# The opening of the first feed-forward stage: operand blocks one at a time, and both modulation vectors summed on the tensor engine

## The chip, the cores and the metric

The kernel runs on one core of a Trainium2 chip, in one launch. Its time is the device time of that launch in microseconds (us), the median of three runs. Five engines work side by side, each through a queue of its own in a fixed order, and wait for one another by semaphores: PE (TensorE, matrix products; its weight loads are shown as PEld), DVE (VectorE), ACT (ScalarE), POOL (GpSimd) and SP, which here issues the transfers (DMA) from the chip's memory.

## The reference

One residual block (feed-forward, mixer, feed-forward, modulated by a condition vector `c`) is followed by two layers of another kind. Only the beginning matters here, up to the first products of the first feed-forward stage, `swiglu`:

```python
cond = jax.nn.silu(c)                                   # 1 x 1024
mod = cond @ w_ada[l] + b_ada[l]                        # 9 vectors of 1024
sh1, sc1, gt1, ... = split(mod, 9)
u = modulate(rmsnorm(h, g_norm_ffn1), sh1, sc1)         # rmsnorm(h) * (1 + sc1) + sh1
h = h + 0.5 * gt1 * swiglu(u, w_ffn1_in, w_ffn1_out)    # 256 tokens, 1024 -> 2 x 2816 -> 1024
```

`w_ada` is 1024 x 9216: each of its nine vectors takes 4 MB of weights, all read once.

## The kernel before

**Layout.** The tokens (256) lie along the free axis, the 1024 features in 8 blocks `k` of 128 partitions: `hT[:, k]` is 128 x 256. A 32-bit product is made of three products of split operands: every operand `x` becomes `hi = round(x)` (ACT, `S.copy`) and `lo = x - hi` (DVE), and `mm3` adds `hi*hi`, `hi*lo` and `lo*hi` in PSUM (lines 249 to 251). `split` (line 254) is that pair. Weights are `hl` (hi and lo halves), activations `xh`, `xl`.

**The first feed-forward stage** (`ffn`) multiplies `u` by `w_ffn1_in`, in 11 column blocks `j` of 2 x 256 columns. Each `j` has two sums in PSUM (`pp[j][s]`), and after the last `k`: ACT makes `sa = silu(a)`, DVE `g = b * sa`, and `split` makes `gh`, `gl`. For `j` of 3 and above the weights come as two 1 MB tiles (`raw`, five buffers) and are split in four pieces of 128 x 1024 (`hl`, six buffers).

**The opening** (`begin`) is different, since at the start nothing is there yet: the transfers of `c`, `x` and weights, the norm of `x` and the first two modulation vectors (shift `ada(0)`, scale `ada(1)`) all stand ahead of the first product. It takes the first three column blocks `j` = 0, 1, 2 together, in six PSUM banks (named `mm` for `j` = 0 and `first` for 1 and 2), and walks over the feature blocks in five groups, `CUTS` = (0), (1, 2), (3, 4), (5, 6), (7). For a group, `prepare` does the following, a group ahead of its products: shift by PE (`ada(0)`: eight matmuls at line 334 with 32 identical columns each, a copy by ACT, then the sum of the four rows by one matmul for a block at line 343), scale by DVE (`ada(1)`: one multiply with a running sum over 128 x 1024 for each block, line 354), `u = hT * r` (DVE), `u * (1+scale) + shift` (ACT), `split` of `u`, and the split of three weight pieces. `r` is the reciprocal root of the mean square of each token, made by `first_rstd`.

**What sets the order.** The code is written in the order of the program, and a scheduler of the kernel's language reorders it for each engine when it is built. `tc.issue_after(x)` keeps what follows behind `x`. On the chip the order of each engine's queue is then fixed. The transfers all go through SP's queue, and wait there for a free buffer. `busy(n)` are products of an identity that nobody reads.

Of the kernel before, what the change touches and what calls it, by code (L numbers as in the profile page):

```python
# [8 lines left out]
F32 = mybir.dt.float32  # L9
F32R = mybir.dt.float32r  # L10
BF16 = mybir.dt.bfloat16
# [95 lines left out]
def _cols(v):  # L107

    return np.ascontiguousarray(np.asarray(v).reshape(-1, P).T)
# [9 lines left out]
def layout(inputs):  # L119
# [5 lines left out]
    o["c_cols"] = _cols(a["c"])  # L125
    o["positions"] = np.ascontiguousarray(a["positions"])
    o["w_ada0"] = _panels(a["w_ada"][0][:, :D], P)
    o["w_ada1"] = np.ascontiguousarray(a["w_ada"][0].T[D:2 * D].reshape(KB, P, D))
    o["w_ada"] = np.ascontiguousarray(
        a["w_ada"][0].T[2 * D:].reshape(7, 4, 2, P, D).transpose(0, 1, 3, 2, 4))  # L130
    o["b_ada"] = _cols(a["b_ada"][0])
    o["gains"] = np.concatenate([_cols(a[k]) for k in
                                 ("g_norm_ffn1", "g_norm_mix", "g_norm_ffn2", "g_final")], 1)
# [41 lines left out]
def body(tc, A, out, dbg=None, stop=None):  # L175
# [3 lines left out]
    with ctx:  # L179
# [67 lines left out]
        def mm3(o, wh, wl, xh, xl, first, last):  # L247

            PE.matmul(o, wh, xh, start=first, stop=False)  # L249
            PE.matmul(o, wh, xl, start=False, stop=False)  # L250
            PE.matmul(o, wl, xh, start=False, stop=last)  # L251
# [46 lines left out]
        ccol = load("c_cols", [P, KB], pool=adap)  # L298
        hT = ctile([P, KB, T], name="hT")
        for i in range(2):  # L300
            nc.sync.dma_start(out=hT[:, 4 * i:4 * i + 4], in_=A["xT"][:, 4 * i:4 * i + 4])
        mats = load("c_mats", [P, 385], ap=A["c_mats"][:, :385])
        ident, perm, mean64 = (mats[:, i * P:(i + 1) * P] for i in range(3))
        part = mats[:, 384:385]
# [9 lines left out]
        b_ada = load("b_ada", [P, 72], pool=adap)  # L314
        gains = load("gains", [P, 32])
        identb = ctile([P, P], BF16, "identb")
# [3 lines left out]
        CUTS = [(0, 1), (1, 3), (3, 5), (5, 7), (7, 8)]  # L320

        def ada(i):

            mod = mods[:, i * 8:i * 8 + 8]
            for a, b in CUTS if i < 2 else [(a, a + 2) for a in range(0, KB, 2)]:
                n, c = b - a, slice(a, b)
                if i == 0:
                    raw = wp.tile([P, 2048], F32, name="raw", tag="raw", bufs=RAW)
                    raw = raw[:, :n * D].rearrange("p (j k n) -> p j k n", j=n, k=KB)
                    nc.sync.dma_start(out=raw, in_=A["w_ada0"][a:b].rearrange("j p k n -> p j k n"))  # L330
                    p = bank("w", "ada")
                    for k in range(KB):
                        r = k % 4 * 32
                        mm = PE.matmul(p[r:r + 32, :n * P], ccol[:, k:k + 1].to_broadcast([P, 32]), raw[:, :, k],
                                       start=(k < 4), stop=(k >= 4))
                    row = tmp0.tile([P, T], F32, name="ar", tag="nt", bufs=2)
                    S.copy(row[:, :n * P], p[:, :n * P])
                    if a == 0:
                        with tc.issue_after(mm.ins):
                            busy(6, "mm")  # L340
                    p = bank("st", "adac")
                    for j in range(n):
                        mm = PE.matmul(p[:, j:j + 1], row[:, j * P:(j + 1) * P], part, start=(j == 0), stop=(j == n - 1))
                    if a == 0:
                        with tc.issue_after(mm.ins):
                            busy(19, "mm")
                    yield
                    V.tensor_tensor(out=mod[:, c], in0=p[:, :n], in1=b_ada[:, c], op=ALU.add)
                    yield
                    continue  # L350
                raw = raw_tile(A["w_ada1"][a:b].rearrange("j p n -> p j n") if i == 1 else A["w_ada"][i - 2, a // 2], n, D)
# [117 lines left out]
        def first_rstd():  # L469

            ss = bank("st", "ss")
            for m in range(KB):
                sq = tmp0.tile([P, T], F32, name="sq", tag="sq", bufs=4)
                if m % 2:
                    V.tensor_tensor(out=sq, in0=hT[:, m], in1=hT[:, m], op=ALU.mult)
                else:
                    S.activation(out=sq, in_=hT[:, m], func=AF.Square)
                r = m % 4 * 32
                PE.matmul(ss[r:r + 32, :T], ones[:, :32], sq, start=(m < 4), stop=(m >= 4))
            sb = tmp0.tile([P, T], F32, name="sr", tag="nt", bufs=2)  # L480
            S.copy(sb, ss[:, :T])
            ss = bank("w", "ss")
            for t in range(2):
                PE.matmul(ss[:, t:t + 1], sb[:, t * P:(t + 1) * P], part, start=(t == 0), stop=(t == 1))
            return Norm().rstd(D, 1e-6, ss)

# [9 lines left out]
        def begin(pool, start, pq, i, uh, ul, win):  # L496

            r = pool.tile([P, T], F32, name="r1")
            V.tensor_copy(r, first_rstd())
            u = pool.tile([P, KB, T], F32, name="u")  # L500
            pp = {}
            for j in range(1, 3):
                pp[j] = [bank(f"b{j}", "first", pq).rearrange("p (a t) -> p a t", a=2) for s in range(2)]
            ws = {}

            def prepare(t):
                k0, k1 = CUTS[t]
                ks, n = range(k0, k1), k1 - k0
                drain(start[0], 1)
                with tc.issue_after(next(start[1]).ins):  # L510
                    drain(start[0], 1)
                raw = []
                for j0, j1 in ((0, 2), (2, 3)):
                    x = wp.tile([P, 2048], F32, name="raw", tag="raw", bufs=RAW)[:, :(j1 - j0) * n * 512]
                    nc.sync.dma_start(out=x.rearrange("p (j k n) -> p j k n", k=n, n=256),
                                      in_=win[j0:j1, :, :, k0:k1].rearrange("j x p k n -> p (j x) k n"))
                    x = x.rearrange("p (j x k n) -> p j x k n", x=2, k=n, n=256)
                    raw += [x[:, j] for j in range(j1 - j0)]
                with (tc.issue_after(ws[t - 1][1].ins) if t else ExitStack()):
                    for k in ks:  # L520
                        V.tensor_tensor(out=u[:, k], in0=hT[:, k], in1=r, op=ALU.mult)

                def modulate():
                    for k in ks:
                        S.activation(out=u[:, k], in_=u[:, k], func=AF.Identity, bias=col(i, k), scale=col(i + 1, k))
                        done = split(uh[:, k], ul[:, k], u[:, k])
                    return done

                def convert():
                    hl = [hl_tile(F32R)[:, :n * 1024].rearrange("p (i x k n) -> p i x k n", i=2, x=2, k=n) for j in range(3)]  # L530
                    for j in range(3):
                        done = split(hl[j][:, 0], hl[j][:, 1], raw[j])
                    ws[t] = hl, done[1]
                    return done

                order = [convert, modulate] if t < len(CUTS) - 1 else [modulate, convert]
                done = order[0]()
                with tc.issue_after(done[0].ins), tc.issue_after(done[1].ins):
                    order[1]()

            prepare(0)
            pp[0] = [mmtile() for s in range(2)]
            for t, (k0, k1) in enumerate(CUTS):
                if t < len(CUTS) - 1:
                    prepare(t + 1)
                for j in range(3):
                    for k in range(k0, k1):
                        for s in range(2):
                            for x in range(2):
                                w = [ws[t][0][j][:, y, x, k - k0, s * P:(s + 1) * P] for y in range(2)]  # L550
                                mm3(pp[j][s][:, x], *w, uh[:, k], ul[:, k], k + x == 0, k == KB - 1 and x == 1)
            return pp

        def ffn(f, nrm, i, side, n_in, n_out, lead, then, pq, start=None):
            with tc.tile_pool(name=f, bufs=1, reuse_waits="tile") as pool:
# [5 lines left out]
                if start:  # L561
                    done = begin(pool, start, pq, i, uh, ul, win)
                else:
                    first = [weights(win[0, x], KB, 256, "k") for x in range(2)]
                    done[0] = [bank("mm", "la"), bank("b", "lb", pq), bank("mm", "lc"), bank("b", "ld", pq)]
                    r = lead_in(nrm, i, lead, first, done[0])
                for j in range(NJ):
                    if j == 5 and start:
                        start[2]()
# [1336 lines left out]
```

## Time and profile before

| | us |
|---|---|
| three runs | 1131.39, 1131.30, 1129.21 (median 1131.3) |
| the profiled execution, its own time | 1133.06 |
| its span, first to last instruction | 1131.3 |
| mean granted TensorE clock | 0.989 |
| first product of the opening starts | 19.11 |
| first product of `j` = 3 starts, the opening's last behind it | 64.97 |

All times below are us from the start of the span. In a row of the timeline stand the start, the time until the last instruction of the row has ended, the engine, the line, the operation, the output and its inputs, the shape, and how many; in brackets how long the engine had been idle before, and what ended it. Matmuls overlap, so the time between two starts is what one costs, not the length of one. In a row of the windows stand the stretch, its length, the busy time of the engines with the number of instructions, the granted TensorE clock (1.00 is 2.4 GHz, 0.50 is 1.2 GHz), the busy share of the DMA engines and their GB/s. A 32-bit matmul that is not split takes two records in the trace, so `x16` for the eight matmuls at line 334.

### The profile page before, as it was taken

How to read it: one execution, taken by the hardware profiler on the slowest of the kernel's cores; microseconds unless marked ns; L12 is line 12 of the kernel's file. 1: busy time of each engine (PE TensorE's matmuls, PEld its weight loads, DVE VectorE, ACT ScalarE, POOL GpSimd, SP SyncE). 2: the span in 40 equal slices, each digit the busy share in tenths (PEclk: the TensorE clock that was granted, in tenths of full speed). 3: DMA queues.
4: the chain of work that ended last, by engine and by line, in shares of the span. 5: the costliest groups of instructions: out<-in, count | busy, mean ns of one | idle time of the engine just before them, and what ended most of it. 6: DMA issues, size and time to landing. Idle time of an engine off the chain costs nothing. (4 is left out here: it accounts for less than half of the span.)

```text
span 1131.3 us, 20262 instructions
## 1 busy us (share of the span) xinstructions
PE 1097.8 (97%) x8303; PEld 914.7 (81%) x8303; DVE 710.7 (63%) x1378; ACT 505.0 (45%) x924; POOL 40.4 (4%) x50
## 2 busy tenths in 40 slices
PE   7999999999999999999999999999999999899995
PEld 4999999999899999999998889545449888854442
DVE  5688878787997875555577854631248875352124
ACT  4464444454554554444556543322247843332122
POOL 0000000100000200000120000000001000000000
PEclk9899999999999999999999999999999999999998
DMA  8898778846884645544565347599864536879971
GB/s 317 295 385 319 271 259 318 283 163 240 320 307 168 215 165 181 181 134 169 182 208 182 145 150 283 205 384 387 342 208 154 180 131 197 324 253 387 397 264 39
DMA packets 77062, 274.16 MB, mean 242 GB/s; under 512 B 7841, under 2 KB 9761, under 8 KB 62370
## 3 DMA queue, kind: packets, MB, share of 16 engines
q1 hardware_dynamic: 76962, 272.79, 66.4%
q8 instruction: 67, 1.10, 0.4%
q14 instruction: 33, 0.27, 0.1%
HBM read 271.73 MB, written 1.05 MB: 241 GB/s over the span
## 5 line engine op out<-in xcount | busy, mean ns | idle before, releaser
L254 DVE TENSOR_TENSOR hl<-raw,hl 128x1024 fp32r<-128x1024 f32 (+5 forms) x267 | 293.5, 1108 | 122.7 <-ACT hl L254 121.6
L254 ACT CAST hl<-raw 128x1024 fp32r<-128x1024 f32 (+5 forms) x267 | 253.6, 958 | 241.4 <-PE mm L251 163.7
L249 PE MATMUL mm<-xh,hl 128*128 128x256 f32 x896 | 255.7, 286 | 2.4 <-ACT xh L254 1.7
L251 PE MATMUL mm<-xh,hl 128*128 128x256 f32 x896 | 255.6, 285 | 0.0
L250 PE MATMUL mm<-xl,hl 128*128 128x256 f32 x896 | 254.3, 284 | 0.0
L249 PEld LDWEIGHTS mm<-xh,hl 128*128 128x128 f32 x896 | 169.7, 190 | 5.2 <-ACT xh L254 2.1
L250 PEld LDWEIGHTS mm<-xl,hl 128*128 128x128 f32 x896 | 170.7, 191 | 2.3 <-issue 1.8
L251 PEld LDWEIGHTS mm<-xh,hl 128*128 128x128 f32 x896 | 170.8, 191 | 1.1 <-issue 1.0
L249 PE MATMUL mm<-gh,hl 128*128 128x256 f32 x352 | 99.3, 282 | 0.0
L250 PE MATMUL mm<-gl,hl 128*128 128x256 f32 x352 | 99.2, 282 | 0.0
L251 PE MATMUL mm<-gh,hl 128*128 128x256 f32 x352 | 99.2, 282 | 0.0
L1706 PE MATMUL gu<-hl,xg 128*64 128x512 f32 x208 | 98.8, 600 | 0.0
L1706 PE MATMUL gu<-raw,xg 128*64 128x512 f32 x192 | 91.4, 605 | 0.0
L354 DVE SCALAR_TENSOR_TENSOR raw<-raw,cond 128x1024 f32<-128x1024 f32 x64 | 76.6, 1219 | 9.3 <-DMA raw<-in_w_ada_dram 9.3
L1742 DVE SCALAR_TENSOR_TENSOR ysl<-dn,gsl,ysh 128x512 fp32r<-128x512 f32 x32 | 23.9, 750 | 75.5 <-ACT ysh L1741 75.5
L250 PEld LDWEIGHTS mm<-gl,hl 128*128 128x128 f32 x352 | 67.0, 190 | 0.0
L249 PEld LDWEIGHTS mm<-gh,hl 128*128 128x128 f32 x352 | 67.0, 190 | 0.0
L251 PEld LDWEIGHTS mm<-gh,hl 128*128 128x128 f32 x352 | 67.0, 190 | 0.0
L1706 PE MATMUL gu<-rawe,xg 128*64 128x512 f32 x112 | 53.9, 610 | 0.0
L1741 ACT ACTIVATE ysh<-dn,gsl 128x512 fp32r<-128x512 f32 x32 | 22.0, 687 | 55.4 <-PE dn L1739 55.4
L1706 PEld LDWEIGHTS gu<-raw,xg 128*64 128x64 f32 x192 | 24.3, 139 | 26.8 <-issue 26.5
L1706 PEld LDWEIGHTS gu<-hl,xg 128*64 128x64 f32 x208 | 25.6, 136 | 23.5 <-issue 21.8
(537 smaller groups left out, 2275.2 us busy)
## 6 DMA issues: line engine op xcount, KB each, us to landing
raw<-in_w_ffn_in_dram SPq DMA_DIRECT2D x41, 1024.0 KB, 4.9
raw<-in_w_ada_dram SPq DMA_DIRECT2D x34, 1024.0 KB, 5.8
raw<-in_w_in_dram SPq DMA_DIRECT2D x34, 1024.0 KB, 5.0
hl<-in_gate_up_dram SPq DMA_DIRECT2D x26, 1024.0 KB, 8.1
raw<-in_gate_up_dram SPq DMA_DIRECT2D x24, 1024.0 KB, 9.3
raw<-in_w_ffn_out_dram SPq DMA_DIRECT2D x32, 704.0 KB, 4.3
rawe<-in_gate_up_dram SPq DMA_DIRECT2D x14, 1024.0 KB, 8.8
raw<-in_w_out_dram SPq DMA_DIRECT2D x12, 1024.0 KB, 4.9
```

Source lines behind the costliest of these rows:

```text
L249: PE.matmul(o, wh, xh, start=first, stop=False)
L250: PE.matmul(o, wh, xl, start=False, stop=False)
L251: PE.matmul(o, wl, xh, start=False, stop=last)
L254: return S.copy(hi, x), V.tensor_tensor(out=lo, in0=x, in1=hi.bitcast(F32), op=ALU.subtract)
L354: V.scalar_tensor_tensor(out=w, in0=w, scalar=1.0, in1=cond, op0=ALU.mult, op1=ALU.mult, accum_out=mod[:, a + j:a + j + 1])
L1706: mm = PE.matmul(p[i * CAP:(i + 1) * CAP], xg[:, k, s], w[i][:, k % 4], start=(k == 0), stop=(k == KB - 1))
L1741: made = S.activation(out=ysh[:, c], in_=p, func=AF.Copy, scale=gc)
L1742: mark[0] = made, V.scalar_tensor_tensor(out=ysl[:, c], in0=p, scalar=gc, in1=ysh[:, c].bitcast(F32), op0=ALU.mult, op1=ALU.subtract)
```

## The change

The opening now takes one feature block a step, eight steps in all, and both vectors of a block are summed on the tensor engine:

- **Transfers.** `c_mats`, `c_cols`, `b_ada` and `gains` are one array, `head` (254 KB). The shift and scale weights of a block are one array, `w_ada01[k]` (1 MB, 2 x 128 columns for each of eight `x`), and the three weight pieces of a block are one transfer (768 KB). Both are loaded two blocks ahead.
- **Modulation.** `modulation_rows(k)` is the eight matmuls, now always 256 wide (shift and scale side by side), and the ACT copy; `modulation_columns(k)` the two matmuls into one column each, and two small DVE operations. The eight long DVE operations of `ada(1)` are gone.
- **Operand.** `u = hT * (1+scale) * r` is one DVE operation (`product`); `modulate` adds the shift in making `xh` (ACT) and `xl` (DVE). The separate ACT operation for `u` is gone. `convert(k)` splits three pieces of 128 x 512.
- **Start.** 20 products of a tile of ones stand at the head of PE's queue; of the products that nobody reads, the ones behind the first block's sums go from 25 to 10. The squares have eight buffers (four before), six of the eight are made by ACT.

```diff
+        warm = ctile([P, P], BF16, name="identb")
+        G.memset(warm, 1.0)
...
+        p = bank("mm", "warm")
+        for i in range(20):
+            PE.matmul(p[:, :P], warm, warm, start=True, stop=True)
...
+            def load(k):
+                raw[k] = [wp.tile([P, 2048], F32, name="raw", tag="raw", bufs=RAW) for x in range(2)]
+                a, b = raw[k]
+                nc.sync.dma_start(out=a.rearrange("p (k n) -> p k n", k=KB), in_=A["w_ada01"][k])
+                nc.sync.dma_start(out=b[:, :1536].rearrange("p (j n) -> p j n", n=256), in_=win[0:3, :, :, k].rearrange("j x p n -> p (j x) n"))
+
+            def modulation_rows(k):
+
+                p = bank("w", "ada")
+                for x in range(KB):
+                    c = x % 4 * 32
+                    mm = PE.matmul(p[c:c + 32, :2 * P], ccol[:, x:x + 1].to_broadcast([P, 32]), raw[k][0][:, x * 2 * P:(x + 1) * 2 * P],
+                                   start=(x < 4), stop=(x >= 4))
+                row[k] = tmp0.tile([P, T], F32, name="ar", tag="nt", bufs=2)
+                S.copy(row[k], p[:, :2 * P])
+                return mm
...
+                for i in range(2):
+                    mm = PE.matmul(p[:, i:i + 1], row[k][:, i * P:(i + 1) * P], part, start=(i == 0), stop=(i == 1))
+                V.scalar_tensor_tensor(out=mods[:, 8 + k:9 + k], in0=p[:, 1:2], scalar=gains[:, k:k + 1], in1=gb[:, k:k + 1],
+                                       op0=ALU.mult, op1=ALU.add)
+                V.tensor_tensor(out=mods[:, k:k + 1], in0=p[:, 0:1], in1=b_ada[:, k:k + 1], op=ALU.add)
...
+            with tc.issue_after(mm.ins):
+                mm = modulation_rows(0)
+            with tc.issue_after(mm.ins):
+                busy(2, "mm")
+                rb = rows_to(bank("mm", "rb")[:, :T], rs)
+                mm = modulation_columns(0)
+            with tc.issue_after(mm.ins):
+                busy(8, "mm")
+            first = product(0, rb)
+            with tc.issue_after(first.ins):
+                V.tensor_copy(r, rb)
+                convert(0)
+            load(1)
+            modulate(0)
...
+            for k in range(KB):
+                if k + 2 < KB:
+                    load(k + 2)
+                more = k + 1 < KB
+                if k == 0:
+                    modulation_rows(1)
+                mm = products(k, 0)
+                if more:
+                    with tc.issue_after(mm.ins):
+                        modulation_columns(k + 1)
+                    ready = product(k + 1, r)
+                    with tc.issue_after(ready.ins):
+                        convert(k + 1, range(1))
+                    done = modulate(k + 1)
+                    with tc.issue_after(done.ins):
+                        convert(k + 1, range(1, 3))
+                mm = products(k, 1)
+                if k + 2 < KB:
+                    with tc.issue_after(mm.ins):
+                        modulation_rows(k + 2)
+                products(k, 2)
```

How the instructions stand on the engines, first ACT where the opening ends and `j` = 3 begins. Before: the last pieces of the opening's weights (`raw_559`, `raw_561`), then the four pieces of `j` = 3 (`hl_722`, `hl_725` of its first tile, `hl_730`, `hl_733` of its second), and `sa` of the six finished sums (`mm_224`, `mm_225`, `first_155` to `first_158`).

```order
L254 CAST hl_569<-raw_561 128x512
L254 CAST hl_722<-raw_720 128x1024
L254 CAST hl_725<-raw_720 128x1024
L254 CAST hl_730<-raw_728 128x1024
L591 ACTIVATE sa_684<-mm_224 128x256
L591 ACTIVATE sa_690<-mm_225 128x256
L254 CAST hl_733<-raw_728 128x1024
L254 CAST gh_113<-g_685 128x256
```

Now, the same place: `hl_664` is the opening's last block, `hl_772`, `hl_775`, `hl_780`, `hl_783` are the four pieces of `j` = 3, and `mm_220`, `mm_221`, `first_222` to `first_225` the six sums.

```order
L251 CAST hl_664<-raw_578 128x512 x3
L603 ACTIVATE sa_734<-mm_220 128x256
L603 ACTIVATE sa_740<-mm_221 128x256
L251 CAST hl_772<-raw_770 128x1024
L251 CAST gh_129<-g_735 128x256
L251 CAST gh_129<-g_741 128x256
L603 ACTIVATE sa_746<-first_222 128x256
L603 ACTIVATE sa_752<-first_223 128x256
L251 CAST hl_775<-raw_770 128x1024
L251 CAST hl_780<-raw_778 128x1024
```

Before, three of the four pieces of `j` = 3 stood ahead of the first `sa`; now the first stands behind two `sa`, and the third (`hl_780`) behind four `sa` and two `gh`. DVE's queue at that place, now:

```order
L251 TENSOR_TENSOR hl_665<-raw_578,hl_664 128x512 x3
L604 TENSOR_TENSOR g_735<-mm_220,sa_734 128x256
L604 TENSOR_TENSOR g_741<-mm_221,sa_740 128x256
L251 TENSOR_TENSOR hl_772<-raw_770,hl_772 128x1024
L251 TENSOR_TENSOR gl_130<-g_735,gh_129 128x256
L251 TENSOR_TENSOR gl_130<-g_741,gh_129 128x256
L604 TENSOR_TENSOR g_747<-first_222,sa_746 128x256
L604 TENSOR_TENSOR g_753<-first_223,sa_752 128x256
L251 TENSOR_TENSOR hl_775<-raw_770,hl_775 128x1024
L251 TENSOR_TENSOR gl_130<-g_747,gh_129 128x256
L251 TENSOR_TENSOR gl_130<-g_753,gh_129 128x256
```

Behind these stand two more `g` and then the `lo` of `hl_780`. Before, the `lo` of `hl_722`, `hl_725` and `hl_730` all stood ahead of the first `g`. PE's queue where `j` = 3 begins, now (its first sum `mm_792` takes `hl_772` and `hl_780` in turn, its second `mm_793` `hl_775` and `hl_783`):

```order
L248 MATMUL first_225<-xh_124,hl_665 128x256
L246 MATMUL mm_792<-xh_124,hl_772 128x256
L247 MATMUL mm_792<-xl_125,hl_772 128x256
L248 MATMUL mm_792<-xh_124,hl_772 128x256
L246 MATMUL mm_793<-xh_124,hl_775 128x256
L247 MATMUL mm_793<-xl_125,hl_775 128x256
L246 MATMUL mm_792<-xh_124,hl_780 128x256
L247 MATMUL mm_792<-xl_125,hl_780 128x256
L248 MATMUL mm_793<-xh_124,hl_775 128x256
L246 MATMUL mm_793<-xh_124,hl_783 128x256
L247 MATMUL mm_793<-xl_125,hl_783 128x256
L248 MATMUL mm_792<-xh_124,hl_780 128x256
```

Ten products of `j` = 3 stand ahead of the first one that needs the `lo` of `hl_780`; the other 86 of the block behind it. From the end of the first feed-forward stage on, every engine has the same order in both programs.

## Rows read from the trace of the kernel before

**Rows 1.** Windows of all engines, a stretch behind the opening.
```profile
60.00:160.00 100.00, 100.00 (x839) 100.00 (x839) 87.44 (x163) 50.12 (x85) 0.00 (x0) 1.00 0.82 311
```
**Rows 2.** Windows of PE alone, the opening and its slow stretch.
```profile
19.11:64.97 45.86, 44.05 (x367) 0.93 0.88 333
...
28.20:35.00 6.80, 6.80 (x39) 0.50 1.05 403
```
**Rows 3.** Timeline of PE in the opening.
```profile
19.11 0.51 PE L249 MATMUL mm<-xh,hl 128*128 128x256 f32 x2 [0.28 <-ACT xh L254]
...
40.99 0.40 PE L249 MATMUL first<-xh,hl 128*128 128x256 f32 x2
41.32 1.07 PE L334 MATMUL ada<-raw,k_c_cols 128*32 128x256 f32 x16
42.32 0.39 PE L250 MATMUL mm<-xl,hl 128*128 128x256 f32 x1
...
42.90 0.58 PE L343 MATMUL adac<-k_c_mats,ar 128*128 128x1 f32 x4
43.35 0.37 PE L251 MATMUL mm<-xh,hl 128*128 128x256 f32 x1
...
47.86 0.28 PE L249 MATMUL first<-xh,hl 128*128 128x256 f32 x1
...
50.73 0.28 PE L249 MATMUL first<-xh,hl 128*128 128x256 f32 x1
...
64.97 0.28 PE L249 MATMUL mm<-xh,hl 128*128 128x256 f32 x1
```
**Rows 4.** Windows of PE, single microseconds around idle stretches.
```profile
26.00:27.00 1.00, 0.14 (x1) 1.00 1.05 430
...
614.00:615.00 1.00, 0.00 (x0) 1.00 0.58 104
...
717.00:718.00 1.00, 0.78 (x4) 0.85 0.00 0
...
721.00:722.00 1.00, 1.00 (x8) 0.95 0.00 0
```
**Rows 5.** Timeline ahead of the first product, and one stretch much later.
```profile
3.45 3.78 PE L312 MATMUL cb<-hl,ones 1*128 1x512 f32 x4 [3.45 <-ACT hl L308]
...
9.77 0.76 DVE L475 TENSOR_TENSOR sq<-hT 128x256 f32<-128x256 f32 x2 [0.66 <-PE ss L479]
...
13.16 0.16 DVE L420 TENSOR_SCALAR v<-ss 128x2 f32<-128x2 f32 x1 [0.98 <-PE ss L484]
...
14.16 1.22 PE L437 MATMUL rb<-k_c_mats,rs 128*128 128x128 f32 x4
...
17.91 1.28 DVE L254 TENSOR_TENSOR hl<-raw,hl 128x512 fp32r<-128x512 f32 x2
...
711.29 0.61 PE L437 MATMUL acc<-k_c_mats,rs 128*128 128x128 f32 x4
```
**Rows 6.** Timeline of first uses of what the transfers bring.
```profile
5.82 0.72 ACT L477 ACTIVATE sq<-hT 128x256 f32<-128x256 f32 x2 [2.32 <-DMA hT<-in_xT_dram]
...
7.69 0.23 DVE L317 CAST identb<-k_c_mats 128x128 bf16<-128x128 f32 x1 [1.11 <-DMA k_c_mats<-in_c_mats_dram]
...
12.32 1.14 ACT L254 CAST hl<-raw 128x512 fp32r<-128x512 f32 x2 [0.27 <-DMA raw<-in_w_ffn_in_dram]
```
**Rows 7.** Timeline of ACT and DVE where `j` = 3 is made ready.
```profile
61.80 0.87 ACT L591 ACTIVATE sa<-mm 128x256 f32<-128x256 f32 x2
...
62.56 1.04 ACT L254 CAST hl<-raw 128x1024 fp32r<-128x1024 f32 x1
63.52 0.41 ACT L254 CAST gh<-g 128x256 fp32r<-128x256 f32 x1
...
61.93 1.23 DVE L254 TENSOR_TENSOR hl<-raw,hl 128x1024 fp32r<-128x1024 f32 x1 [1.40 <-ACT hl L254]
63.08 0.75 DVE L592 TENSOR_TENSOR g<-mm,sa 128x256 f32<-128x256 f32 x2
```

More of the change, by code (lines that the diff above doesn't have):

```diff
@@ L313, in body @@
             V.tensor_copy(cond[:, i * 512:(i + 1) * 512], cb)
-        b_ada = load("b_ada", [P, 72], pool=adap)
-        gains = load("gains", [P, 32])
-        identb = ctile([P, P], BF16, "identb")
+        identb = warm
         V.tensor_copy(identb, ident)
         mods = ctile([P, 72], name="mods")
-        CUTS = [(0, 1), (1, 3), (3, 5), (5, 7), (7, 8)]
         def ada(i):
             mod = mods[:, i * 8:i * 8 + 8]
[L325 to L351, printed above, removed]
+            for a in range(0, KB, 2):
+                b, n, c = a + 2, 2, slice(a, a + 2)
+                raw = raw_tile(A["w_ada"][i - 2, a // 2], n, D)
                 for j in range(n):
@@ L467, in norm_mod @@
                                        op0=ALU.add, op1=ALU.subtract)
[L469 to L485, printed above, removed]
         def drain(it, n):
@@ L493, in chain, with begin @@
                 yield from it
-        def begin(pool, start, pq, i, uh, ul, win):
+        def begin(pool, pq, uh, ul, win):
             r = pool.tile([P, T], F32, name="r1")
[L499 to L551, printed above, removed]
@@ new lines, in product, with modulate @@
+            def product(k, rows):
+                u[k] = pool.tile([P, T], F32, name="u", tag="u", bufs=3)
+                return V.scalar_tensor_tensor(out=u[k], in0=hT[:, k], scalar=col(1, k), in1=rows, op0=ALU.mult, op1=ALU.mult)
+            def modulate(k):
+                S.activation(out=uh[:, k], in_=u[k], func=AF.Identity, bias=col(0, k))
+                return V.scalar_tensor_tensor(out=ul[:, k], in0=u[k], scalar=col(0, k), in1=uh[:, k].bitcast(F32),
+                                              op0=ALU.add, op1=ALU.subtract)
@@ new lines, in begin @@
+            load(0)
+            gb = pool.tile([P, KB], F32, name="gb1")
+            V.scalar_tensor_tensor(out=gb, in0=b_ada[:, 8:16], scalar=1.0, in1=gains[:, 0:8], op0=ALU.add, op1=ALU.mult)
+            ss = bank("st", "ss")
+            for m in range(KB):
+                sq = pool.tile([P, T], F32, name="sq0", tag="sq0", bufs=8)
+                if m in (1, 3):
+                    V.tensor_tensor(out=sq, in0=hT[:, m], in1=hT[:, m], op=ALU.mult)
+                else:
+                    S.activation(out=sq, in_=hT[:, m], func=AF.Square)
+                c = m % 4 * 32
+                PE.matmul(ss[c:c + 32, :T], ones[:, :32], sq, start=(m < 4), stop=(m >= 4))
@@ new lines, in begin @@
+            sb = tmp0.tile([P, T], F32, name="sr", tag="nt", bufs=2)
+            S.copy(sb, ss[:, :T])
+            ss = bank("mm", "ss")
+            for t in range(2):
+                mm = PE.matmul(ss[:, t:t + 1], sb[:, t * P:(t + 1) * P], part, start=(t == 0), stop=(t == 1))
+            v = Norm().variance(D, 1e-6, ss)
+            rs = rsqrt(v, 2, tmp0)
+            with tc.issue_after(mm.ins):
[4 more added lines that the diff above has]
+                mm = modulation_columns(0)
@@ L561, in ffn @@
                 if start:
-                    done = begin(pool, start, pq, i, uh, ul, win)
+                    done = begin(pool, pq, uh, ul, win)
                 else:
```

44 lines of the change are left out of this document (29 added, 15 removed).

## Prediction

> **What bounds the kernel now.** I read the windows by stage first, then PE's timeline in the opening, then what the other engines do around its two ends. Behind the opening PE has no idle time: in 60 to 160 us it is busy for 100.00 of 100.00 us, with DVE at 87% and DMA at 0.82 of its engines [rows 1]. So whatever the opening gains or loses goes into the end almost one for one, and I compare one instant: the first product of `j` = 3, at 64.97, and then how that block runs.
>
> The opening takes 45.86 us from its first product at 19.11 [rows 2, 3]. In PE's plain stretches a product of 128x256 costs 0.1196 us: 24 of them lie between 47.86 and 50.73 [rows 3]. The opening has 8 blocks x 12 sums x 3 = 288, so 34.4 us. The shift's eight 256-wide matmuls cost 1.09 us (the product before starts at 40.99 with its pair, which ends its turn at 41.23; the next starts at 42.32), the column matmuls 0.45 (42.90 to 43.35) [rows 3]. Three such groups and two narrower ones, of which one lies in the opening, make about 5.5 us. That leaves 45.9 - 34.4 - 5.5 = 6.0 us. 3.4 of them are the stretch from 28.20 to 35.00, in which the granted clock is 0.50, the lower level, 1.2 GHz: 6.80 us at half speed [rows 2]. The rest is waiting, most of it around 26 us, where PE is busy for 0.14 us of one [rows 4].
>
> **The change, part by part.**
>
> *Until the first product.* Before, the last squares end at 9.77 + 0.76 = 10.53, since the second four wait for buffers, and the variance starts at 13.16, 2.63 us later [rows 5]. Now eight buffers free the squares: they wait for the second half of `x` alone. Before, 1.25 MB had landed when `identb` was made at 7.69, the first half of `x` at 5.82 [rows 6]; now the second half is behind 1.31 MB that start one issue earlier, so about 7.4. Four squares on ACT at 0.36 each (two in 0.72) [rows 6] give 8.9. From there two bounds, for PE's clock in these microseconds. At the lower level: variance at 8.9 + 2.63 = 11.5; the first block's rows, twice 1.09, until 13.7; `rb` 1.22 [rows 5] and two idle products ahead of it, 1.5 together, columns 0.5: 15.7. At the upper level PE's parts halve (`rb` costs 0.61 at 711.29 against 1.22 at 14.16 [rows 5]): variance at 10.4, rows until 11.6, columns ready at 12.6. Then DVE in its order: two small operations 0.3 (as `v`, 0.16 each), `u` 0.4 and the copy of `r` 0.35 (as the squares, two in 0.76), three `lo` at 0.64 (two of 128x512 in 1.28) [rows 5], `xl` 0.4, together 3.4. Six `hi*hi` products (0.7 us) run ahead of `xl`. So the first product counts as started at 15.7 + 3.4 - 0.7 = 18.4 or at 15.3, against 19.11. ACT's casts of the first weights (before at 12.32 [rows 6], now behind 0.2 MB more and an issue less) fit under both. I take 17.0, the middle: a gain of 2.1 us, with bounds of 0.7 and 3.8.
>
> The Trainium skill, "TensorE: Matmul & The Clock Gate" (section "Part 1: The HAM clock gate"), says that the throttled clock is the default and that activity releases it. By that rule the 20 products at the head, with the sums for `cond` right behind them, would bring the upper level before the chain, and 15.3 would be the figure. This trace does not bear it out so simply: the sums for `cond` keep PE busy for 3.78 us without a gap [rows 5], and the rows behind them still cost twice what they cost at the upper level.
>
> *The opening itself.* 34.4 us of products stay. The sums of the modulation become seven full groups (the eighth, block 0's, stands ahead): 7 x (1.09 + 0.45) = 10.8. The gap before a block's first product needs the chain from the columns: small operations 0.3, `u` 0.4, `xh` 0.4, `xl` 0.4, with the steps from engine to engine under 2 us; behind it stand 14 to 21 products (1.7 to 2.5 us), so I add 0.8 for the tightest blocks, 5 and 6. Sum 46.0, as long as before's 45.86 [rows 2]: the modulation on PE takes the room that the slow stretch and the waits leave. If the clock comes up only behind the first products, that is up to 1.7 more; I take 0.5. DVE loses eight long operations, and that is worth nothing, since PE is the bound. The transfers bring the same bytes, 1.8 MB for a block; at the 403 GB/s of the slow stretch [rows 2] that is 4.5 us, under the 5.8 of a step, and they are issued two blocks ahead. `j` = 3 can begin at 17.0 + 46.0 + 0.5 = 63.5, 1.5 us earlier.
>
> *The first products of `j` = 3.* Here the order turns against it. Before, the pieces `hl_722` and `hl_730` of its first sum stood in ACT's and DVE's queues ahead of `sa` and `g` of the six sums; at 64.97 PE went on without a gap [rows 3]. Now `sa_734` and `sa_740` stand ahead of the first piece, and they wait for sums that end only within block 7: `mm_221` at its 14th product, 1.55 + 0.28 = 1.8 us behind the block's start. From there ACT's chain, by the pitches of [rows 7] (`sa` 0.35, a 128x1024 cast 0.96, `gh` 0.32): `sa_740` 2.2, `hl_772` 3.2, two `gh` and two `sa` 4.5, `hl_775` 5.4, `hl_780` 6.4, two `gh` 7.0, two `sa` 7.65. DVE's chain (a `lo` of 128x1024 1.15, two `g` or two `gl` 0.67): `hl_772` from 3.2 to 4.4, two `gl` and two `g` 5.8, `hl_775` 6.95, two `gl` 7.6, two `g` behind the last `sa` 8.2, `hl_780` 9.4. PE is through block 7 at 36 x 0.12 = 4.3 and has ten products of `j` = 3 that it may do before the `lo` of `hl_780`: 5.5. So it stands still for 9.4 - 5.5 = 3.9 us. Bounds: 3.6 by the shortest pitches all along; nothing, if I have the queues wrong. I take 3.8. The other 86 products then find everything ready, and DVE is free about 9 us before block 4.
>
> *The clock behind it.* In 4.9 us PE does ten products. After a thin stretch around 26 us the clock fell to 0.50 at 28.2 for 6.80 us [rows 2, 4]; it fell again within 717 to 718 and came back at the beginning of 721 to 722 [rows 4], some 3.4 us; after a clean gap of one to two microseconds at 614 it stayed at 1.00 [rows 4]. So 0, 1.7 or 3.4 us. The new wait is thinner and longer than the one at 26 us, so I expect a fall; part of the slow stretch will lie in the wait itself, where it costs nothing, so I take 1.7.
>
> *The small things* (one array for four, `gb`, the fill of the ones tile, other banks) stand off the path at the start, behind transfers: nothing. If the fill came late, the 20 products would push the sums for `cond`, which have 1.5 us of room before the squares.
>
> **The sum.** -2.1 (start) + 0.1 (opening) + 0.5 (clock at its beginning) + 3.8 (wait) + 1.7 (clock behind it) = +4.0 us. The profiled execution took 1133.06 us, so 1137.1 there; it lies 1.8 above the median of the runs, 1131.3, so I forecast 1135.3 for the median. A difference under 0.2% (2.3 us) is what a measurement of this kernel can't tell from none.
>
> **The rivals.**
>
> *Not slower: the clock stays up.* If the early products bring PE to the upper level and it is still there in block 3, the opening starts at 15.3 and nothing follows the wait: -3.8 + 0.1 + 3.8 = +0.1, or 1131.4, and about 1130 if the transfers land a microsecond earlier than I put them. It decides at one point, whether a thin stretch of 4.9 us with ten products brings the clock down. For it speaks 614 us, against it 26 and 717 [rows 4]. 28%.
>
> *Faster: the wait isn't there.* If ACT and DVE reach `hl_780` before PE needs it (the sums of `j` = 0 ending much earlier than I think, or the pieces taking far less than their rows), the early start remains: -2.1 + 0.1 + 0.5 = -1.5, or 1129.8, and 1127.6 with the early bound. Against it stands the order of both queues, which no timing undoes; for it only that I count from pitches of another place. 13%.
>
> *Slower still: the lower level at both ends.* Start at 18.4, the first 3.4 us of products at half speed, the wait, and 6.8 us slow behind it: -0.7 + 0.1 + 1.7 + 3.9 + 3.4 = +8.4, or 1139.7. 9%.
>
> *The change doesn't do what it says*, that is, the products wait for transfers after all, since a block's weights come in runs of 1 KB. At 300 GB/s in place of 403, a step would take 6.0 us in place of 5.8: 1.6 us more over eight, 1136.9, inside the forecast's range. 4%, counted with it.
>
> The forecast itself, 1133.6 to 1138, has the rest, 50% with the last. Faster by over 0.2%: the second rival's better part and a little of the first, 13%. Within 0.2%: most of the first, the rest of the second and an edge of the forecast, 28%. Slower: 59%. For eight of ten the range goes from 1129.5 to 1139.5.
>
> **What would show it.** First product (as counted above) between 15 and 18.5; blocks 5.8 us apart, without PE idle time over 0.6 us; PE standing from about 0.4 us behind the opening's last product until the `lo` of `hl_780` ends, 3.5 to 4 us in pieces, with ACT and DVE named as releasers; the granted clock at 0.50 within 5 us of it. The prediction is wrong if PE goes from block 7 into `j` = 3 without a wait, or if the opening's first product comes before 14.

## The result, and the profile after

| | kernel before | changed kernel |
|---|---|---|
| median of 5 runs each, us | 1131.3 | 1139.22 (1136.3 to 1140.26) |
| ratio, 95% interval | | 1.0063 [1.0046, 1.0080] |
| once more, as run 4 below (5 runs, 15 of before) | 1131.57 | 1137.6, ratio 1.0052 [1.0034, 1.0069] |
| span of the profiled execution | 1131.3 | 1137.4 |

Slower, by 6 to 8 us. (The profiled execution of the kernel before took 1.8 us more than its median, that of the changed kernel is its median; so the traces have 6.1 us to explain and not 7.9.) From the opening's second block on PE now has no idle time, as it had none before behind the opening [rows 1]. Windows of PE in the changed kernel (stretch, length, busy time, granted clock, DMA share, GB/s): the opening from block 1 on, the first products of `j` = 3, those behind them, and the second half of the stage (the products of `gh` and `gl`, line 618).

```profile
26.50:67.50 41.00, 41.00 (x369) 1.00 0.82 286
68.17:73.29 5.12, 2.75 (x12) 0.83 0.60 195
73.29:78.37 5.08, 5.08 (x24) 0.50 0.83 299
166.80:227.40 60.60, 60.60 (x531) 1.00 0.87 305
```

The wait is in the second line and the slow clock in the third. The fourth holds a gain that the prediction has no term for; the kernel before needs this for the same 531 records:

```profile
157.30:220.70 63.40, 63.40 (x531) 1.00 0.84 291
```

PE's timeline at the start of the changed kernel, against [rows 3, 5]:

```profile
1.00 2.31 PE L307 MATMUL warm<-identb 128*128 128x128 bf16 x20 [1.00 <-POOL identb L302]
3.48 3.78 PE L313 MATMUL cb<-hl,ones 1*128 1x512 f32 x4 [0.17 <-ACT hl L309]
...
11.80 1.93 PE L468 MATMUL ada<-raw,head 128*32 128x256 f32 x16
...
13.85 1.17 PE L411 MATMUL rb<-head,rs 128*128 128x128 f32 x4
...
19.02 0.58 PE L247 MATMUL mm<-xl,hl 128*128 128x256 f32 x1 [0.34 <-DVE xl L490]
...
19.96 1.94 PE L468 MATMUL ada<-raw,head 128*32 128x256 f32 x16
...
24.00 0.37 PE L247 MATMUL first<-xl,hl 128*128 128x256 f32 x1
24.21 0.28 PE L248 MATMUL first<-xh,hl 128*128 128x256 f32 x1
...
27.95 1.07 PE L468 MATMUL ada<-raw,head 128*32 128x256 f32 x16
```

The same sixteen records of line 468 take 1.93 and 1.94 us at 11.80 and 19.96, and 1.07 at 27.95: until about 24.0 PE runs at the lower level, although the granted clock is shown as 1.00 there. Ahead of the clock's first recorded change, the level is read from the length of equal work, not from that column.

PE where `j` = 3 begins; before, it went on without a gap [rows 3]:

```profile
68.05 0.28 PE L248 MATMUL first<-xh,hl 128*128 128x256 f32 x1
68.17 0.28 PE L246 MATMUL mm<-xh,hl 128*128 128x256 f32 x1
...
69.20 0.39 PE L246 MATMUL mm<-xh,hl 128*128 128x256 f32 x1 [0.46 <-ACT hl L251]
...
70.14 0.39 PE L246 MATMUL mm<-xh,hl 128*128 128x256 f32 x1 [0.44 <-ACT hl L251]
...
70.82 0.38 PE L248 MATMUL mm<-xh,hl 128*128 128x256 f32 x1 [0.18 <-DVE hl L251]
72.25 0.58 PE L246 MATMUL mm<-xh,hl 128*128 128x256 f32 x1 [1.04 <-ACT hl L251]
...
73.29 0.58 PE L248 MATMUL mm<-xh,hl 128*128 128x256 f32 x1 [0.25 <-DVE hl L251]
73.67 0.41 PE L246 MATMUL mm<-xh,hl 128*128 128x256 f32 x1
```

And DVE ahead of it, against [rows 7]:

```profile
65.66 0.90 DVE L604 TENSOR_TENSOR g<-mm,sa 128x256 f32<-128x256 f32 x2
67.07 1.23 DVE L251 TENSOR_TENSOR hl<-raw,hl 128x1024 fp32r<-128x1024 f32 x1 [0.51 <-ACT hl L251]
68.22 0.76 DVE L251 TENSOR_TENSOR gl<-g,gh 128x256 fp32r<-128x256 f32 x2
68.89 0.75 DVE L604 TENSOR_TENSOR g<-first,sa 128x256 f32<-128x256 f32 x2
69.56 1.22 DVE L251 TENSOR_TENSOR hl<-raw,hl 128x1024 fp32r<-128x1024 f32 x1
70.69 0.75 DVE L251 TENSOR_TENSOR gl<-g,gh 128x256 fp32r<-128x256 f32 x2
71.36 0.75 DVE L604 TENSOR_TENSOR g<-first,sa 128x256 f32<-128x256 f32 x2
72.02 1.22 DVE L251 TENSOR_TENSOR hl<-raw,hl 128x1024 fp32r<-128x1024 f32 x1
```

The third `lo` ends at 73.24, and the product that needs it starts at 73.29. Ten products (1.2 us) in 5.12 us: a wait of 3.9. Its idle pieces add up to 2.4 only; in the rest a product stands alone and takes its whole length, 0.28 to 0.58 us, where in a stream one starts every 0.12. PE was never still for over 1.04 us, and yet the clock fell.

### The profile page after: what moved, and what is told of

It reads as the page before. It is cut to its first block, busy times and chain, and to the rows that moved or that the text cites. A ratio compares the mean times of both kernels' runs of the same rounds, so it can differ in the third digit from the quotient of the medians.

```text
span 1137.4 us, 20386 instructions
## 1 busy us (share of the span) xinstructions
PE 1106.7 (97%) x8372; PEld 918.2 (81%) x8372; DVE 703.0 (62%) x1371; ACT 503.5 (44%) x930; POOL 40.0 (4%) x51
## 5 line engine op out<-in xcount | busy, mean ns | idle before, releaser
L328 DVE SCALAR_TENSOR_TENSOR raw<-raw,cond 128x1024 f32<-128x1024 f32 x56 | 66.9, 1218 | 8.7 <-DMA raw<-in_w_ada_dram 8.7
```

Of the source, the lines that this page charges most:

```text
L328: V.scalar_tensor_tensor(out=w, in0=w, scalar=1.0, in1=cond, op0=ALU.mult, op1=ALU.mult, accum_out=mod[:, a + j:a + j + 1])
```

## The experiments

Theory A: the time is lost at the two ends of the opening, at the lower level in block 0 and in the wait at `j` = 3 with the slow clock behind it. Theory B: it is the opening itself, the sums on PE, and the wait only fills time that PE loses anyway. Ratios are to runs of the kernel before on the same chip.

**1. The pieces of `j` = 3 ahead of the sums again.**

```diff
                     done = begin(pool, pq, uh, ul, win)
+                    early = [weights(win[3, x], KB, 256, made=2 - x) for x in range(2)]
...
+                            with ExitStack() as behind:
+                                for x in (early[1].last if start and j < 3 else ()):
+                                    behind.enter_context(tc.issue_after(x.ins))
```

> The changed kernel, with the first three weight pieces of j = 3 put ahead of the six finished sums on ACT and DVE, as they stood before the change; nothing else moves. Theory A (the queues of ACT and DVE make PE wait): the ten products of j = 3 run without a gap, the wait of 3.9 us is gone, the clock doesn't fall at 72 us (24 products at 0.213 us there against 0.12, 2.2 us), together -6.1 us: about 1133 against 1139.2. If the products of the stage's second half (166 to 227 us) go back from the pitch of 0.1145 us that they have in the changed kernel to the 0.1197 of the kernel before, 2.8 of it are lost: 1136. Theory B (the extra time is the opening's own, the sums on PE and the start, and the wait at j = 3 only fills time that PE loses anyway behind it): less than 2 us, 1137 to 1139.

Measured: 1134.35, ratio 1.0010 [0.9997, 1.0023], where the changed kernel has 1.0052, so 4.8 us less: theory A, though not the whole 6.1 that it expected. PE's first line at `j` = 3, then two windows:

```profile
69.01 0.39 PE L246 MATMUL mm<-xh,hl 128*128 128x256 f32 x1 [1.24 <-DVE g L608]
```
```profile
68.00:69.00 1.00, 0.00 (x0) 1.00 1.06 451
...
70.00:76.00 6.00, 6.00 (x52) 1.00 0.88 301
```

Another wait takes the place of the first: `j` = 3 writes into the PSUM bank that `g` of `j` = 0 frees, and `g` now stands behind three pieces on DVE. It is 1.24 us in one piece, and the clock stays. So 3.9 + 2.2 became 1.24 of idle time. The second half kept its gain.

**2. The wait left, PE kept busy in it.**

```diff
...
+                            if start and j == 3:
+                                for x, n in (((2, 9), (4, 4)), ((1, 9), (2, 20), (4, 6)))[s]:
+                                    with tc.issue_after(made[at + x].ins):
+                                        busy(n)
```

(`made` lists the products in the order in which they are written.)

> The changed kernel, with 50 of the products that nobody reads (128x128) put between the first ten products of j = 3, where PE stands; the order of ACT and DVE stays. Theory A: the wait stays (the last of the ten products still ends 3.9 us late, since it waits for DVE), but the clock stays at 1.00 behind it: -2.2 us, about 1137. If the fall of the clock isn't due to the thin stretch, the granted clock is 0.50 again from 72 us on and the time is the same, 1139, or up to 1 us more by the added products. Theory B: the same time.

Measured: 1138.13, ratio 1.0039 [1.0027, 1.0052]. That is 1.5 us under the changed kernel's 1.0052 where 2.2 were expected, and the intervals overlap; the profile decides:

```profile
67.87:73.33 5.46, 4.84 (x57) 1.00 0.58 198
73.33:78.00 4.67, 4.67 (x42) 1.00 0.88 279
```

The product behind the first ten is no earlier than in the changed kernel (5.46 us behind the first, against 5.12), but PE is at the upper level there, with 42 records in 4.67 us where the changed kernel has 24 in 5.08. Wait and clock are two costs, 3.9 and 2.2 us, and PE's lack of work in the stretch brings the second.

**3. The same order put into the kernel before.**

```diff
-                        wa, wb = [weights(win[j, x], KB, 256) for x in range(2)]
+                        late = start and j == 3
+                        wa, wb = [weights(win[j, x], KB, 256, made=0 if late else 2) for x in range(2)]
+                        for w, i, n in ((wa, 0, 1), (wa, 1, 3), (wb, 0, 5)) if late else ():
+                            with tc.issue_after(sas[min(n, 3)].ins), tc.issue_after(gs[n].ins):
+                                w.make(i)
...
```

(`sas` and `gs` list the `sa` and `g` instructions, as they are written.)

> The kernel before, with the weight pieces of j = 3 put behind the finished sums on ACT and DVE, as the changed kernel has them: first piece behind sa of j = 0, second and third behind sa of j = 1, the third piece's lo behind the last g. The opening stays as it was. Theory A: the lo of the third piece ends at about 69.6 (g of j = 0 at 62.3, then two g 0.75, three lo at 1.15, five gl and four g at 0.34), while PE has done its ten products of j = 3 by 66.2: a wait of 3.4 us, and 0 to 2.2 us of slow clock behind it: +3.4 to +5.6 us over the kernel before. Theory B (the wait at j = 3 only fills time that PE loses anyway): within 1 us of the kernel before.

Measured: 1137.97, ratio 1.0053 [1.0036, 1.0071], +6.4 us between the medians, slightly over theory A's upper end. Its windows, from the first product of `j` = 3:

```profile
65.57:70.42 4.85, 2.82 (x12) 0.85 0.50 159
70.42:75.71 5.29, 5.29 (x25) 0.50 0.64 217
```

Ten products in 4.85: a wait of 3.65, and 24 to 25 products at the lower level behind it, 2.3 us. The old opening with the new order at its end costs as much as the whole change. Theory B, in which the wait only fills time that PE loses anyway, is out. One count in the profiles puts the three runs side by side, from the first product of `j` = 3 to the first of the second half: 91.7 us in the kernel before and 97.9 with the order put into it; 98.0 in the changed kernel, 96.4 with PE kept busy (run 2), 92.0 with the pieces ahead (run 1, counted behind its wait).

**4. The changed kernel once more.** No edit.

> The changed kernel as it is, once more, to stand beside the others on one chip. All theories: 0.4% to 0.8% over the kernel before, as in its first five runs (ratio 1.0063). If it is nearer than that (within 0.25%), the first measurement took in something of the day or the chip, and the gains of the other experiments, measured against 1139.2, are to be cut by as much.

Measured: 1137.6, ratio 1.0052 [1.0034, 1.0069].

**5. The sums on PE done twice.**

```diff
-                for x in range(KB):
+                for x in [*range(KB)] * (2 if k else 1):
```

> The changed kernel, with the eight matmuls of the modulation's rows done twice for blocks 1 to 7 (the second pass writes the same sums again). If PE bounds the opening: 7 x 8 x 0.122 = +6.8 us, the step of a block 7.0 in place of 6.1. If the transfers or DVE bounded it: the added matmuls hide in PE's gaps, +0 to 2 us.

Measured: 1141.32, ratio 1.0082 [1.0060, 1.0104], +3.7 us against 4, between the two answers. The opening itself speaks for PE: it is busy for 41.00 of 41.00 us again,

```profile
26.50:67.50 41.00, 41.00 (x435) 1.00 0.82 285
```

and from the third group of sums to the opening's last product it took 44.7 us in place of 40.1 (six groups twice: 0.77 for each, against 0.98 expected). The time of the whole run tells less, for the order at its end moved with the edit: on ACT three casts of the 128x1024 pieces now start ahead of the first `sa` (65.73 and 67.41 against 69.31), and PE goes into `j` = 3 without a wait or a slow clock. What that gave back was lost again in the second half, which took 65.7 us from its first product to its last (59.7 in run 4), with one wait of 2.14 us and the lower level from 206.2 to 209.5 behind it:

```profile
205.07 0.35 PE L246 MATMUL mm<-gh,hl 128*128 128x256 f32 x1 [2.14 <-DVE hT L618]
```

**6. More idle products ahead of block 0.**

```diff
-                busy(8, "mm")
+                busy(24, "mm")
```

> The changed kernel, with 24 in place of 8 products that nobody reads behind the columns of block 0, as the kernel before had 19. Theory A: the upper level comes before the opening's first products in place of at 24.0 us; the products between 19.0 and 24.0 then take half: -2.4 us, less what the added products push the first ones behind (16 x 0.055 to 0.125, of which 0.8 fall into gaps: 0.1 to 1.2 us): 1136.8 to 1138. Theory B (the clock is not what costs at the beginning): 1139 to 1140.5, later by the added products.

Measured: 1136.72, ratio 1.0026 [1.0014, 1.0038]. PE's timeline:

```profile
20.15 0.41 PE L247 MATMUL mm<-xl,hl 128*128 128x256 f32 x1
...
20.58 0.28 PE L246 MATMUL mm<-xh,hl 128*128 128x256 f32 x1
```

The upper level is there at 20.4, the first product behind `xl` comes 1.1 us later than in the changed kernel, and the opening ends at 67.14 in place of 68.05 (or 67.93 in run 4). The direction is theory A's. The size is not settled: by the ratios it is 2.9 us (1.0026 against 1.0052), in the profile 0.8 to 0.9, where 1.2 to 2.4 were expected; the profile is of the slowest of the twelve runs.

**7. No early products.** The loop of 20 is taken out.

> The changed kernel without the 20 products at the head of PE's queue. Theory A: they don't bring the upper level in this kernel (the matmuls behind them run at half rate until 24.0 us), so nothing changes: 1139 within 0.5 us, the first product at 19.0 as counted in the changed kernel's profile. The rival, that they carry part of the later rise: the upper level comes later than 24.0 us, up to 3 us of products at half rate more, 1139.5 to 1141.

Measured: 1135.4, ratio 1.0019 [1.0005, 1.0034], lower than either side expected. PE's timeline:

```profile
18.93 1.90 PE L465 MATMUL ada<-raw,head 128*32 128x256 f32 x16
20.76 0.38 PE L247 MATMUL mm<-xl,hl 128*128 128x256 f32 x1
20.98 0.28 PE L248 MATMUL mm<-xh,hl 128*128 128x256 f32 x1
```

The upper level comes at 20.8, 3.2 us earlier *without* them; the opening ends at 65.85. Runs 5 and 8 to 10 show how far this is chance.

**8. Without the early products, two pieces ahead of `j` = 0 and the third ahead of `j` = 1.**

```diff
+                    early = [weights(win[3, x], KB, 256, made=2 - 2 * x) for x in range(2)]
...
+                            if start and j == 1 and s == 0:
+                                early[1].make(0)
```

> The changed kernel without the 20 early products, and with two weight pieces of j = 3 ahead of the sums of j = 0 on ACT and DVE, the third ahead of those of j = 1. With three ahead of j = 0, PE still stood 1.24 us at j = 3, for the PSUM bank that g of j = 0 frees. Theory A: that wait goes to 0.5 us or less, there is no slow clock behind it, and the opening ends where it did without the early products, at 65.9 in place of 68.1: in the profile j = 3 runs from 66.0 without a gap over 0.5, and the time is 7 to 8 us below the changed kernel's, within 0.2% of the kernel before or 1 us under it. Theory C (the gain without the early products was chance in when the upper level comes): the opening ends at 67.5 to 68, the time is 5.5 us below the changed kernel.

Measured: 1135.19, ratio 1.0028 [1.0012, 1.0044], 2.4 us under the changed kernel; theory A had 7 to 8, theory C 5.5, so both miss. The opening ends at 65.69 and the clock stays, as theory A said, but the fourth piece fell behind two long modulation steps on DVE, and PE waited later within `j` = 3 (and once more at 206.47, for 0.97 us):

```profile
73.94 0.39 PE L246 MATMUL mm<-xh,hl 128*128 128x256 f32 x1 [0.76 <-DVE g L607]
...
75.14 0.39 PE L248 MATMUL mm<-xh,hl 128*128 128x256 f32 x1 [0.70 <-DVE hl L251]
```

**9. The fourth piece ahead of `j` = 2 too** (the edit is against run 8).

```diff
-                            if start and j == 1 and s == 0:
-                                early[1].make(0)
+                            if start and s == 0 and j in (1, 2):
+                                early[1].make(j - 1)
```

> The changed kernel without the 20 early products, with two weight pieces of j = 3 ahead of the sums of j = 0 on ACT and DVE, the third ahead of those of j = 1 and the fourth ahead of those of j = 2. With the fourth left to its place, it fell behind two long modulation steps on DVE, and PE waited 0.76 and 0.70 us within j = 3. Theory A: these two waits go, j = 3 runs from 66 with waits under 0.6 us in all, no slow clock; the first stage ends at 221.5 or earlier in the profile (before 220.7 + 0.48, changed 227.5), and the time is within 0.15% of the kernel before, on either side. Rival: the waits only move on to j = 4, and the time stays at 0.25% above the kernel before.

Measured: 1133.36, ratio 1.0008 [0.9991, 1.0024]: within the 0.15% of theory A, though the interval reaches beyond. Both waits are gone, but the rival has its part: one of 1.25 us came in `j` = 5, behind other DVE work.

```profile
93.49 0.39 PE L248 MATMUL mm<-xh,hl 128*128 128x256 f32 x1 [1.25 <-DVE hl L251]
```

In this execution the upper level came at 24.1 only, again without early products, and the opening ended at 67.54. That is what theory C of run 8 had said, and run 8, with 65.69, had spoken against. The twelve runs lie between 1128.6 and 1138.1, so one profile is one draw.

**10 to 12. The pitch of the second half.** A product there costs 0.1200 us in the kernel before and 0.1134 in the changed one (means of starts from 166 to 198 us), for the same 528 products. What differs, by the program's allocations, is where the operands lie: before, `hl` and `gh` begin at multiples of 128 bytes in each partition; in the changed kernel `hl` begins 64 off one, as the constants take 320 bytes more. Ten: the changed kernel with 64 bytes free ahead of `gh` and `gl`. Eleven: the kernel before with the same gap. Twelve: the kernel before with a second gap ahead of `ones`, so that `hl`, `gh`, `xh` and `xl` lie as in the changed kernel.

```diff
+                if start:
+                    pool.tile([P, 16], F32, name="pad")
                 gh = pool.tile([P, FB, T], F32R, name="gh")
```

> The changed kernel, with 64 bytes left free ahead of gh and gl: both then begin at the same distance from a multiple of 128 bytes as the weights hl, as in the kernel before. Theory D: the pitch in the stage's second half goes from 0.1134 to 0.1200, the stretch takes 63.4 us in place of 60.6, and the time rises by 2.8 us, to 0.75% to 0.85% over the kernel before. Theory E: pitch and time as in the changed kernel (0.5% to 0.6% over the kernel before).

> The kernel before, with 64 bytes left free ahead of gh and gl (and so all that the first stage's pool holds lies 64 bytes further in each partition); no instruction is added or moved. In the kernel before, gh and the weights hl both begin at multiples of 128 bytes, and the 528 products of the stage's second half have a pitch of 0.1200 us; in the changed kernel gh still does, hl begins 64 bytes off one, and the pitch is 0.1134. Theory D (the place of the two operands against each other sets the pitch): the pitch goes to 0.1134 from 158 to 221 us, that stretch takes 60.6 us in place of 63.4, and the time falls by 2.8 us (0.25%). Theory E (the pitch comes from something else, the transfers or the other engines at that time): 0.1200 as before and the same time.

> The kernel before with two gaps of 64 bytes, one ahead of the small constants' ones tile (all that is allocated behind it moves by 64 bytes) and one ahead of gh and gl: hl then begins 64 bytes off a multiple of 128, gh at one, xh 64 bytes off and xl at one, all four as in the changed kernel. No instruction is added or moved. With the second gap alone (hl at a multiple of 128, gh 64 off) the pitch went from 0.1200 only to 0.1178 us. Theory D' (the pitch hangs on where both operands lie, not on their distance alone): the pitch goes to 0.1134, the stretch from the last sa to the last hT to 60.6 us in place of 63.4, and the time falls by 2.8 us (0.25%), which would make it faster than both kernels. Theory E' (the changed kernel's pitch has another cause, and the distance decides the rest): the pitch stays at 0.1178 as with one gap, the time 0 to 1 us below the kernel before.

Measured: 1140.29, ratio 1.0081 [1.0068, 1.0095]; 1131.12, ratio 0.9993 [0.9982, 1.0004]; 1132.34, ratio 0.9991 [0.9977, 1.0005]. The stretch in each, in this order:

```profile
164.30:227.70 63.40, 63.40 (x531) 1.00 0.84 294
```
```profile
154.40:216.70 62.30, 62.30 (x531) 1.00 0.86 306
```
```profile
158.20:220.50 62.30, 62.30 (x531) 1.00 0.86 305
```

The gap takes the changed kernel's gain away to the last hundredth (63.40), so theory D is right in that the place sets the pitch. In the kernel before it gives 1.1 us and not 2.8, and the second gap adds nothing: theory D' fails, and which other place matters stays open. Neither of the two is shown to be faster than the kernel before, since both intervals include 1; so no version here is shown to beat both kernels.

Run 10 tells of the start, too. Its instructions there are the changed kernel's, and yet, in PE's timeline and in the window of a first fall:

```profile
11.60 1.07 PE L468 MATMUL ada<-raw,head 128*32 128x256 f32 x16
...
17.12 0.39 PE L247 MATMUL mm<-xl,hl 128*128 128x256 f32 x1 [1.01 <-DVE xl L490]
```
```profile
17.80:21.10 3.30, 3.30 (x23) 0.50 1.04 369
```

Here PE was at the upper level by 11.6, the first product came 1.9 us earlier, and then the clock fell at 17.8 for 3.3 us, behind waits of 0.90 and 1.01 us; the opening ended at 65.57. Run 5, with the same instructions up to 19.86, did likewise a little later: its eight idle products took 0.61 us (1.01 in the changed kernel), and behind waits of 0.90 and 1.02 us the clock fell at 18.4.

```profile
15.42 0.61 PE L346 MATMUL busy<-identb 128*128 128x128 bf16 x8
```
```profile
19.00:20.00 1.00, 1.00 (x7) 0.50 0.96 334
```

In runs 1, 2 and 4, with the same instructions up to there, the upper level came at 22.7, 23.0 and 23.4.

## Why the prediction was right, and where it was not

| step | forecast, us | profile after, us |
|---|---|---|
| start (first product, as counted) | -2.1 (17.0) | -0.8 (19.02 - 0.7 = 18.3) |
| opening, and clock at its beginning | +0.1, +0.5 | +4.0 (18.3 to 68.17 is 49.9, against 45.86) |
| wait at `j` = 3 | +3.8 | +3.9 |
| clock behind it | +1.7 | +2.2 (24 products in 5.08 us, 2.87 at full rate) |
| pitch of the second half | - | -2.8 (60.60 against 63.40) |
| behind the stage | - | -0.6 (1137.4 - 227.4, against 1131.3 - 220.7) |
| sum | +4.0 | +5.9 (spans: +6.1) |

The median, 1139.22, lies above the forecast's own 1133.6 to 1138 and just inside the range of eight in ten; run 4, at +6.0, comes nearer. The -0.6 behind the stage is put down to nothing: from the start of the stage's last product to the end, the 14 profiles lie between 910.4 and 913.2 us.

*The wait* is right in place, size and mechanism. The chain put the third `lo` 9.4 us behind block 7's start; that block's first product starts at 63.70, the `lo` ended at 73.24, 9.5 later. Run 1 takes the wait away, run 3 makes it in the other kernel.

*The clock behind it* fell, as forecast, and cost 2.2 us. It fell in all six profiles in which the whole wait of some 3.9 us came in thin pieces (the changed kernel's two, runs 3, 6, 7 and 10), and in none in which it was filled (run 2) or became one gap of 1.24 us (run 1) or two waits of 0.76 and 0.70 (run 8). So the first rival, in which the clock stays up, is out at the point that it named itself.

*The start* was mis-sized: the middle of the two bounds was taken (17.0), and the profile has the late one (18.3). The rule of the Trainium skill, "TensorE: Matmul & The Clock Gate", section "Part 1: The HAM clock gate", that activity releases the throttle, would have given the early one. The traces agree with it only in part: in runs 5 and 10 PE was at the upper level by 15.4 and 11.6 us, and in the four other executions of the same start the products and sums from 1.0 to 7.3 us left it at the lower one until 22.7 to 24.0.

*The opening* is the term that failed most, by 3.4 us: "if the clock comes up only behind the first products, that is up to 1.7 more; I take 0.5". From 19.02 to 24.00 all of PE's work ran at half rate: that is 2.5 us, over its upper bound too. The rest, 1.4, is the step: five of them from 27.95 to 59.59, by the first rows of line 468, are 6.33 us each, not 5.85 and a tenth. The sums were priced at 1.09 + 0.45; that a product beside them, or at a block's beginning, starts 0.15 to 0.22 us behind the one before in place of 0.12, about five times in a step, was mostly left out. That PE bounds the opening and the transfers don't was right (41.00 of 41.00 us busy, run 5).

*Not foreseen*: the second half's pitch, -2.8, as much as the misses at the start (1.3) and in the opening's step (1.4) together. The forecast's direction stands on the wait and its clock, which alone are as much as the 6.1 us between the spans; the start and the opening (+3.2) and the pitch and the rest (-3.4) cancel. That +4.0 comes as near to +5.9 as it does is luck: misses of opposite sign. The rival "lower level at both ends", held at 9%, had the shape of this profile: start 18.4, slow first products, wait, slow clock behind. Its +8.4 is nearer to the first median's +7.9 than the forecast, and near to what stands behind the wait at `j` = 3 (-0.8 + 4.0 + 3.9 + 2.2 = +9.3) before the pitch takes its part.

## What to carry to other kernels

Where a rewrite removes waits from a stage, read the queues of the engines at its end: finishing work that used to come late can now stand ahead of the next stage's first operands, and the wait, with the clock that falls behind it, can cost more than the stage gained. Don't judge by the longest gap alone whether the clock will hold: the changed kernel lost it with no gap over 1.04 us, and run 1 kept it over one of 1.24. Whether pieces are worse than one gap of the same total isn't shown: single gaps of 2.40 us (run 12) and 2.14 (run 5) had a fall behind them too. And before 2 or 3 us are put down to an edit, compare the pitch of equal products elsewhere in both traces: a change of the layout moved 528 of them by 6%.

## What the runs showed that was not expected

- The pitch of a 128x256 product of split operands, all on chip and without a wait, was 0.1200, 0.1178 or 0.1134 us, by where the operands lie (runs 10 to 12). Shown for 64 bytes more ahead of `gh` and `gl`; the rule behind it isn't.
- The same instructions reached the upper level by 11.6 us in one execution, by 15.4 in another, and at 22.7 to 24.0 in four others; in the first two the clock fell once more, before 19 us; without the 20 early products it came at 20.8, 20.6 and 24.1 (runs 7, 8, 9). Whether these products harm, as the ratio of run 7 would have it, is not settled.
- The kernel before has such a difference too: the slow stretch from 28.20 to 35.00 [rows 2] is absent in run 11, where the waits around 26 us were 0.53 and 0.45 us in place of 1.42 and 0.39, and whose opening ends 2.9 us earlier (61.95 against 64.84). In run 12 there was one wait of 2.40 us there, and the clock fell behind it:

```profile
28.20 0.50 PE L249 MATMUL mm<-xh,hl 128*128 128x256 f32 x2 [2.40 <-ACT xh L254]
```
```profile
28.00:30.00 2.00, 1.79 (x20) 0.99 1.03 398
30.00:32.00 2.00, 2.00 (x11) 0.50 1.05 388
```
